# The delta rule's diagonal blocks inverted row by row on VectorE, and the heads' sums of squares as float32r rows

## The chip, the cores and the metric

The kernel runs on one core of a Trainium2 chip. The metric is the device time of one execution in microseconds (us); the execution before took 1631.58 us, the median of three. A core has the engines TensorE (PE: matrix products, and PEld, its loading of weights), VectorE (DVE), ScalarE (ACT), GpSimd (POOL) and SyncE (SP: it issues the loads of weights from memory). Each engine works through its own queue in a fixed order and waits for others on semaphores. PE writes its products to PSUM, all else lies in SBUF.

## The reference

Two layers of a hybrid block, then a second block of two (dilated attention with a short convolution, a gated feed-forward, retention, a second feed-forward). One sequence of 256 positions, model width 1024, all in float32. The change touches the mixer of the first block's two layers, which run over 16 + 256 = 272 positions:

```python
def gated_deltanet(q, k, v, z, a, b, conv_w, a_log, dt_bias, norm_g):
    qkv = jax.nn.silu(causal_dwconv(jnp.concatenate([q, k, v], axis=-1), conv_w))
    ...
    q = l2_norm(q.reshape(Bsz, T, A_HEADS, A_DK)) * (A_DK ** -0.5)
    k = l2_norm(k.reshape(Bsz, T, A_HEADS, A_DK))
    g = -jnp.exp(a_log.astype(f32)) * jax.nn.softplus(a.astype(f32) + dt_bias.astype(f32))
    ...
    decay = jnp.exp(jnp.where(incl, gcum[..., :, None] - gcum[..., None, :], -jnp.inf))
    kk = jnp.einsum('bhncd,bhnsd->bhncs', kc, kc)
    m = jnp.where(strict, bc[..., None] * kk * decay, 0.0)
    lhs = m + jnp.eye(CHUNK, dtype=f32)
    sol = lax.linalg.triangular_solve(lhs, rhs, left_side=True, lower=True, unit_diagonal=True)
    ...

def dsa_attention(q, k, v, iq, ik, iw, q_norm, k_norm, kidx_norm, cos_a, sin_a, cos_i, sin_i):
    q = apply_rope(rms_norm(q.reshape(Bsz, T, B_HEADS, B_DH), q_norm), cos_a, sin_a)
    k = apply_rope(rms_norm(k.reshape(Bsz, T, 1, B_DH), k_norm), cos_a, sin_a)[:, :, 0]
    ik = apply_rope(rms_norm(ik.reshape(Bsz, T, 1, IDX_DIM), kidx_norm), cos_i, sin_i)[:, :, 0]
    ...
```

So a layer needs, for every position, the sum of squares of 4 query heads and 4 key heads of the delta rule, 4 query heads and one key of the attention, and one index key: 14 sums. And for each of the 4 delta heads it needs the inverse of `I + m`, a unit triangular matrix, in each piece of the sequence. The kernel cuts the 272 positions into segments of 16, 128 and 128.

## The kernel before

**The stream.** Most of the time goes to products of activations with weights in float32r, a form of float32 with fewer bits kept. To keep float32's accuracy, weights and activations are split into a high and a low part, and `mm3` (L279) makes three products per 128 x 128 tile of weights: high x high (L287), high x low (L288), low x high (L289). `dense` (L291) loads weights (`raw`, 2 buffers), splits a block of 1024 columns with `split` (L259: ScalarE writes `whi`, VectorE `wlo`, 4 buffers each), and runs 24 products into one PSUM tile for every 128 output columns.

**The side chains.** Everything else in a mixer is written as generators: `small_chain` (decay gates, the index key), `key_chain` (the attention's key and value), `delta` (L917: `part1`, then `scan`, for the three segments) and `sparse` (top-k selection and attention). `dense` calls `tick` at its fourth tile and after each 128 output columns, and a tick lets every started chain go one step. What a chain issues thus stands in the engines' queues between products of the stream. A scheduler then fixes the order of each engine's queue. The order of the units of a layer is one line:

```python
for name in (begin + " k1 g1 q0 g2 q1 D i0 i1 S kv K v0 b0 v1 b1 g3 z0 z1 g4 g5 g6 g7").split():
```

`D` and `S` start the chains of the delta rule and of the attention, `M` the small chain, `K` the key chain; a chain waits with `until` for what it needs.

**The sums of squares.** `stats` (L493) squares a head on ScalarE (`sqm`, L496) and, two ticks later, multiplies each segment of it with a column of ones, in plain float32: three matmuls of one moving column into one PSUM tile `stat` (L500). The sums land one per partition (per position). A normalised value that is needed as a row across partitions goes through `rowcast` (L363). Each group of sums has its own Newton iteration for the inverse square root (`rsqrt`, L246: one start value and three rounds of three small VectorE instructions, L252 to L256).

**The inverse.** `part1` (L717) makes the decays (L723, L725), the matrix `MT` of a segment for 4 heads (L732, L735), and inverts it by levels: pairs (L739, L740), then two radix-4 steps of 2 and 8 rows (L764 to L776, with a transposition back of `XT` by L752 behind each), then the pair of 32 (L797 to L804), then the pair of 64 (L813, L818). Each product is four plain-fp32 matmuls, one per head. For the 16-row segment there is one radix step and the pair of 8. The 128-row segments are worked on in turn, after the 16-row segment's `scan`.

**How plain fp32 shows.** Each plain-fp32 matmul of the program is two records of the profile, one for each of its passes (a transposition is one). The stream's float32r products are one record.

## Time and profile before

| | |
|---|---|
| three runs | 1629.08, 1631.58, 1631.98 us |
| profiled execution | 1631.2 us, its span 1629.4 us |
| mean granted TensorE clock | 0.991 of full speed |
| PE busy | 1611.3 us, 11806 records |
| DVE busy | 1246.8 us, 2715 records |
| ACT busy | 890.1 us, 1556 records |
| GpSimd busy | 18.0 us |
| stretch read as layer 0's mixer | 25 to 277 us |

The span runs from the first instruction to the last; the execution's own time is a little longer. A row of the timeline gives the start, the duration, the engine, the line, the operation, and the names of what is written and read; equal neighbours are joined (x8). Matmuls are pipelined, so their durations overlap; what one costs is read from the distance of starts. Of the granted clock, 1.00 is the 2.4 GHz level and 0.50 the 1.2 GHz level.

### The profile page before, as it was taken

What the parts mean: (1) busy time and instruction counts of PE and PEld (TensorE: products, weight loads), DVE (VectorE), ACT (ScalarE), POOL (GpSimd) and SP (SyncE); (2) the same over time, 40 slices, a digit from 0 to 9 for tenths busy, and PEclk for the clock granted to TensorE, in tenths of its full rate; (3) what the DMA queues carried; (4) which work ended last, traced back from release to release, by engine and by line L of the source; (5) the groups of instructions that cost most, each with busy time, mean ns of one, the idle gap of its engine ahead of it and who ended that gap; (6) DMA issues with size and microseconds to landing.
All of it is one profiled execution on the core that took longest, in us unless ns stands there. A gap on an engine that the chain in (4) does not pass through costs nothing.

```text
span 1629.4 us, 30001 instructions
## 1 busy us (share of the span) xinstructions
PE 1611.3 (99%) x11806; PEld 1505.1 (92%) x11806; DVE 1246.8 (77%) x2715; ACT 890.1 (55%) x1556; POOL 18.0 (1%) x174
## 2 busy tenths in 40 slices
PE   7999999999999999999999999999999999999999
PEld 7989999999999989999998898899988888899997
DVE  6787568888557797588887649899956767789974
ACT  5665455555445664556665446566644444556652
POOL 0000000000000000000000000000000000000000
PEclk9998999999999999999999999999999999999999
DMA  5431224445553422245555553455555454545553
GB/s 207 155 110 73 104 99 161 169 171 179 169 181 130 155 104 79 79 147 170 193 191 179 200 180 126 160 182 188 185 183 194 158 178 155 174 169 192 190 183 128
DMA packets 38445, 257.89 MB, mean 158 GB/s; under 512 B 4384, under 2 KB 6816, under 8 KB 9120
## 3 DMA queue, kind: packets, MB, share of 16 engines
q1 hardware_dynamic: 37440, 253.79, 45.1%
q8 instruction: 93, 1.52, 0.4%
q10 hardware_dynamic: 864, 2.18, 0.3%
q14 instruction: 48, 0.39, 0.1%
HBM read 254.90 MB, written 1.05 MB: 157 GB/s over the span
## 4 chain that ended last, share of the span: by engine, by line
PE 96%; DVE 2%; ACT 1%; issue 0%; DMA 0%; SPq 0%; DVEq 0%; ACTq 0%
PE psd L289 20%; PE psd L287 19%; PE psd L288 18%; PE pss L285 5%; PE psn L285 5%; PE psd L285 3%; PE pss L289 3%; PE psn L289 3%; PE psn L771 1%; PE stat L500 1%; PE psd L352 1%; PE psd L353 1%; PE psd L354 1%; PE psn L353 1%; PE psn L352 1%; PE psn L354 1%
## 5 line engine op out<-in xcount | busy, mean ns | idle before, releaser
L261 ACT ACTIVATE whi<-raw 128x1024 fp32r<-128x1024 f32 (+1 forms) x487 | 508.3, 1044 | 546.6 <-PE psd L288 285.4
L262 DVE TENSOR_TENSOR wlo<-raw,whi 128x1024 fp32r<-128x1024 f32 (+1 forms) x487 | 585.2, 1202 | 206.9 <-ACT whi L261 202.6
L289 PE MATMUL psd<-x,wlo 128*128 128x256 f32 (+2 forms) x2384 | 682.5, 286 | 0.8 <-DVE wlo L262 0.8
L287 PE MATMUL psd<-x,whi 128*128 128x256 f32 (+2 forms) x2208 | 644.3, 292 | 7.0 <-ACT whi L261 6.3
L288 PE MATMUL psd<-x,whi 128*128 128x256 f32 (+2 forms) x2208 | 631.0, 286 | 0.0
L289 PEld LDWEIGHTS psd<-x,wlo 128*128 128x128 f32 x2384 | 451.9, 190 | 2.1 <-DVE wlo L262 1.3
L287 PEld LDWEIGHTS psd<-x,whi 128*128 128x128 f32 x2208 | 419.5, 190 | 15.7 <-ACT whi L261 6.3
L288 PEld LDWEIGHTS psd<-x,whi 128*128 128x128 f32 x2208 | 420.5, 190 | 3.0 <-issue 1.7
L289 PE MATMUL pss<-ax,wlo 128*128 128x256 f32 (+1 forms) x352 | 99.2, 282 | 0.0
L289 PE MATMUL psn<-ax,wlo 128*128 128x256 f32 (+1 forms) x352 | 99.2, 282 | 0.0
L285 PE MATMUL pss<-ax,whi 128*128 128x512 f32 x264 | 92.5, 394 | 0.0
L285 PE MATMUL psn<-ax,whi 128*128 128x512 f32 x264 | 92.5, 394 | 0.0
L289 PEld LDWEIGHTS psn<-ax,wlo 128*128 128x128 f32 x352 | 66.2, 188 | 0.0
L289 PEld LDWEIGHTS pss<-ax,wlo 128*128 128x128 f32 x352 | 66.2, 188 | 0.0
L285 PE MATMUL psd<-x,whi 128*128 128x512 f32 x176 | 61.7, 393 | 0.0
L285 PEld LDWEIGHTS pss<-ax,whi 128*128 128x128 f32 x264 | 49.6, 188 | 11.6
L285 PEld LDWEIGHTS psn<-ax,whi 128*128 128x128 f32 x264 | 49.6, 188 | 11.5
L389 ACT ACTIVATE gy<-gu,prm 128x256 f32<-128x256 f32 (+1 forms) x88 | 43.6, 500 | 4.0 <-DVE gu L386 3.8
L391 DVE SCALAR_TENSOR_TENSOR gy<-gu,prm,gy 128x256 f32<-128x256 f32 (+1 forms) x88 | 42.5, 485 | 1.7
L390 DVE SCALAR_TENSOR_TENSOR gy<-gu,prm,gy 128x256 f32<-128x256 f32 (+1 forms) x88 | 42.3, 483 | 0.9 <-ACT gy L389 0.9
L386 DVE TENSOR_TENSOR gu<-psd,rB 128x256 f32<-128x256 f32 (+2 forms) x88 | 37.0, 424 | 5.0 <-PE psd L289 3.7
L285 PEld LDWEIGHTS psd<-x,whi 128*128 128x128 f32 x176 | 33.0, 188 | 7.0
(404 smaller groups left out, 2497.2 us busy)
## 6 DMA issues: line engine op xcount, KB each, us to landing
raw<-in_w_up_dram SPq DMA_DIRECT2D x44, 1024.0 KB, 4.8
raw<-in_ffn_w_up_dram SPq DMA_DIRECT2D x44, 1024.0 KB, 4.7
raw<-in_w_in_dram SPq DMA_DIRECT2D x26, 1024.0 KB, 4.8
raw<-in_w_gate_dram SPq DMA_DIRECT2D x16, 1024.0 KB, 4.8
raw<-in_w_down_dram SPq DMA_DIRECT2D x16, 1024.0 KB, 4.9
raw<-in_ffn_w_down_dram SPq DMA_DIRECT2D x16, 1024.0 KB, 4.9
...
```

The source lines that it names most:

```text
L261: self.nc.scalar.activation(hi, src, AF.Copy)
L262: self.nc.vector.tensor_tensor(lo, src, hi.bitcast(F32), OP.subtract)
L285: mm(ps.rearrange("p (a n) -> p a n", a=2), w[0], x, start=first, stop=False)
L287: mm(ps, w[0], hi, start=first, stop=False)
L288: mm(ps, w[0], lo, start=False, stop=False)
L289: mm(ps[:, :n], w[1], hi, start=False, stop=last)
L352: mm(ps[m], h, hi[:, k, :], start=(kk == 0), stop=False)
L353: mm(ps[m], h, lo[:, k, :], start=False, stop=False)
L386: V.tensor_tensor(u[:, 2:2 + n], ps, N.rB, OP.mult)
L389: A.activation(y, u[:, o:o + T], AF.Copy, scale=conv(0, c))
L390: V.scalar_tensor_tensor(y, u[:, o + 1:o + 1 + T], conv(1, c), y, OP.mult, OP.add)
L391: V.scalar_tensor_tensor(y, u[:, o + 2:o + 2 + T], conv(2, c), y, OP.mult, OP.add)
```

## The change

**Sums of squares.** `square_parts` squares a head twice on ScalarE, to float32 and to float32r, and VectorE subtracts for a low part. The sum is then two float32r products of all 272 columns (`sums`), whose stationary matrix is a window of `pick` that has ones in one column and zeros elsewhere: the sum of head `r` lands in row `r` of a PSUM tile, and the other rows get zero added. Three sets a layer collect in the PSUM tile of bank x: `k5` (four keys and the index key), `q4` and `b5` (four attention queries and the attention key). When a set is full, ScalarE copies the rows out, and `columns` transposes the three segments (three transpositions a set). The Newton iterations become two of 15 columns. The index key's and attention key's factors are spread over partitions by `spread` (two float32r products of all-ones) in place of `rowcast`. A new chain `keys` starts with the small chain; the attention key is scaled later, in `sparse`.

**The inverse.** `delta` makes decays and `MT` of all three segments first. The 16 x 16 diagonal blocks of all 12 pairs of segment and head are gathered in one tile (`diag`: a mask, then a reduction on VectorE). `eliminate` scales them 15 times on ScalarE, spreads each column over its block's partitions with three products with the block mask (plain fp32), and runs 15 steps of a multiplication and a subtraction on VectorE, which invert all blocks at once. `part1` then starts from inverted blocks of 16: one radix-4 step of 16 rows and the pair of 64. For the 16-row segment the blocks are the result. The decay gates' sums take three matmuls, not six.

```diff
+    def square_parts(self, src, scale=1.0):
+        T = src.shape[1]
+        sq = self.st.tile([P, T1], F32, tag="sq", name="sqm", bufs=2)[:, :T]
+        hi, lo = self.part(T), self.part(T)
+        self.nc.scalar.activation(sq, src, AF.Square, scale=scale)
+        self.nc.scalar.activation(hi, src, AF.Square, scale=scale)
+        self.nc.vector.tensor_tensor(lo, sq, hi.bitcast(F32), OP.subtract)
+        return hi, lo
+    def sums(self, ps, w, hi, lo, first=True, last=True):
+        self.nc.tensor.matmul(ps, w, hi, start=first, stop=False)
+        self.nc.tensor.matmul(ps, w, lo, start=False, stop=last)
+    def spread(self, ps, cols, segs):
+        ns, T = len(segs), segs[-1][0] + segs[-1][1]
+        ch, cl = self.small(ns, "spr_h", F32R), self.small(ns, "spr_l", F32R)
+        self.nc.vector.tensor_copy(ch, cols)
+        self.nc.vector.tensor_tensor(cl, cols, ch.bitcast(F32), OP.subtract)
+        parts = []
+        for c in (ch, cl):
+            d = self.part(T)
+            for s, (o, n) in enumerate(segs):
+                self.nc.scalar.activation(d[:, o:o + n], self.c["ident"][:, :n], AF.Copy,
+                                          scale=c.bitcast(F32)[:, s:s + 1])
+            parts.append(d)
+        self.sums(ps[:, :T], self.ones, *parts)
...
-    stat = k_.ps("x", "stat")
-    SQ, SK, SA, SKA, SKI = 0, 12, 24, 36, 40
-    V.memset(stat[:, :43], 1.0)
     known = set()
-    def stats(src, rows, at, key):
-        sq = k_.st.tile([P, T1], F32, tag="sq", name="sqm", bufs=3)
-        A.activation(sq[:rows], src, AF.Square)
+    rows = {}
+    def stats(src, row, of, scale=1.0):
+        hi, lo = k_.square_parts(src, scale)
 
         def sums():
-            for s, (o, n) in enumerate(segs):
-                mm(stat[:n, at(s):at(s) + 1], sq[:rows, o:o + n], c["ones"][:rows, 0:1], start=True, stop=True)
-            known.add(key)
-        k_.defer(2, sums)
+            first = of not in rows
+            if first:
+                rows[of] = k_.ps("x", "rows")
+            rows["n", of] = rows.get(("n", of), 0) + 1
+            last = rows["n", of] == int(of[1])
+            k_.sums(rows[of][:, :T], k_.pick[:, P - 1 - row:2 * P - 1 - row], hi, lo, first, last)
+            if last:
+                t = tmp("rows")[:, :T]
+                A.activation(t, rows[of][:, :T], AF.Copy)
+                rows[of] = t
+                known.add(of)
+        k_.defer(3, sums)
+    def columns(of):
+        ps = k_.ps("s")
+        for s, (o, n) in enumerate(segs):
+            tr(ps[:, s * P:(s + 1) * P], rows[of][:, o:o + P], ident)
+        return ps[:, :3 * P].rearrange("p (s c) -> p s c", s=3)[:, :, :int(of[1])]
...
+    def keys():
+        yield from until("k5")
+        u = k_.small(15, "uki", bufs=2)
+        sums = columns("k5")
+        V.tensor_scalar(u[:, :12].rearrange("p (s h) -> p s h", s=3), sums[:, :, :4], 4.0 * EPS, None, OP.add)
+        V.scalar_tensor_tensor(u[:, 12:], sums[:, :, 4], 1.0 / 64.0, S["epu"], OP.mult, OP.add)
+        r = k_.rsqrt(u, 15, "rki")
+        uk = u[:, :12]
+        srk = k_.small(12, "srk", bufs=2)
+        V.tensor_tensor(srk, r[:, :12], uk, OP.mult)
+        yield
+        yield from until("small")
+        ruk = k_.small(12, "ruk")
+        V.reciprocal(ruk, uk)
+        bet = k_.small(12, "bet", bufs=2)
+        V.tensor_tensor(bet, S["beta"], ruk, OP.mult)
+        S["srk"], S["bet"] = srk, bet
+        known.add("bet")
...
+                stats(o, hh, "k5" if which == "k" else "q4")
...
+    diag = quad("vs", 2).rearrange("p h n -> p (h n)")[:, :12 * B].rearrange("p (h r) -> p h r", h=12)
+    slot = {0: 8, 1: 0, 2: 4}
...
+        own = diag[:, slot[s]:slot[s] + 4, :]
+        if s:
+            W = quad("W", 2)
+            V.tensor_tensor(W, MT, mid(c["blk"], 4), OP.mult)
+            V.tensor_reduce(own, W.rearrange("p h (b r) -> p h r b", r=B), AX.X, OP.add)
+        else:
+            G.memset(own, 0.0)
+            A.activation(own[:n], MT[:n], AF.Copy)
...
+    XD = dn.tile([P, 12, B], F32, tag="XD", name="XD")
+    def eliminate():
+        views = []
+        for tag, group in (("od", range(0, 3)), ("vt", range(3, 7)), ("ks", range(7, B - 1))):
+            low, o = quad(tag).rearrange("p h n -> p (h n)"), 0
+            for j in group:
+                m = B - 1 - j
+                views.append(low[:, o:o + 12 * m].rearrange("p (h r) -> p h r", h=12))
+                A.activation(views[j], diag[:, :, j + 1:], AF.Copy, scale=c["idb"][:, j:j + 1])
+                o += 12 * m
+            ps = k_.ps("n")
+            mm(ps[:, :o], c["blk"], low[:, :o], start=True, stop=True)
+            A.activation(low[:, :o], ps[:, :o], AF.Copy)
+            yield
+        V.tensor_copy(XD, mid(c["idb"], 12))
+        Y = quad("Y", 2).rearrange("p h n -> p (h n)")
+        for j in range(B - 1):
+            m = B - 1 - j
+            t = Y[:, :12 * m].rearrange("p (h r) -> p h r", h=12)
+            V.tensor_tensor(t, views[j], XD[:, :, j:j + 1].to_broadcast([P, 12, m]), OP.mult)
+            V.tensor_tensor(XD[:, :, j + 1:], XD[:, :, j + 1:], t, OP.subtract)
+            if j % 3 == 2:
+                yield
...
+    def part1(s):
+        o, n = segs[s]
+        E4, DT, MT = S["E4"], DTs[s], MTs[s]
+        own = XD[:, slot[s]:slot[s] + 4, :]
+        if s:
+            XT, Xm = quad("XT", 2), quad("X", 2)
+            V.tensor_tensor(XT.rearrange("p h (b r) -> p h b r", r=B),
+                            own.unsqueeze(2).to_broadcast([P, 4, NB, B]),
+                            c["blk"].rearrange("p (b r) -> p b r", r=B).unsqueeze(1).to_broadcast([P, 4, NB, B]),
+                            OP.mult)
...
-        yield from until("small", *[(w, hh) for w in "qk" for hh in range(4)])
-        uqk = k_.small(24, "uqk", bufs=2)
-        V.tensor_scalar(uqk, stat[:, :24], 4.0 * EPS, None, OP.add)
-        uk = uqk[:, 12:24]
-        rk = k_.rsqrt(uk, 12, "rk")
-        srk = k_.small(12, "srk", bufs=2)
-        V.tensor_tensor(srk, rk, uk, OP.mult)
-        ruk = k_.small(12, "ruk")
-        V.reciprocal(ruk, uk)
-        bet = k_.small(12, "bet", bufs=2)
-        V.tensor_tensor(bet, S["beta"], ruk, OP.mult)
+        yield from until("bet", "q4")
         epo = k_.small(12, "epo", bufs=2)
-        V.tensor_scalar(epo, uqk[:, 0:12], 16.0 * EPS * 128.0, None, OP.mult)
-        S["srk"], S["bet"], S["epo"] = srk, bet, epo
-        yield
+        V.tensor_scalar(epo.rearrange("p (s h) -> p s h", s=3), columns("q4"), 4.0 * EPS, 16.0 * EPS * 128.0,
+                        OP.add, OP.mult)
+        S["epo"] = epo
+        yield
+        yield from in_turn(decays(0), decays(1), decays(2))
+        yield from eliminate()
         yield from part1(0)
...
-             "M": lambda: k_.start(small_chain()), "K": lambda: k_.start(key_chain())}
+             "M": lambda: (k_.start(small_chain()), k_.start(keys())), "K": lambda: k_.start(key_chain())}
```

**Where the instructions go.** Three places are shown, before and now.

On PE, early in layer 0, the sum of the index key's squares before, as it stands in the stream (`stat` is the tile of sums, `x_...` and `psd` are the stream's):

```order
L288 MATMUL psd<-x_119,whi 128x272
L289 MATMUL psd<-x_119,wlo 128x272
L500 MATMUL stat<-g_77,sqm 16x1
L500 MATMUL stat<-g_77,sqm 128x1 x2
L173 MATMUL pss<-g_77,sacc 16x1
L173 MATMUL pss<-g_77,sacc 128x1 x2
L287 MATMUL psd<-x_98,whi 128x272
L288 MATMUL psd<-x_98,whi 128x272
```

and the end of the first set now, with the low part's product (L279) and the three transpositions (L550, `columns`):

```order
L324 MATMUL psd<-x_103,whi 128x272
L325 MATMUL psd<-x_103,whi 128x272
L279 MATMUL rows<-sqp,pick 128x272
L326 MATMUL psd<-x_103,wlo 128x272
L324 MATMUL psd<-x_106,whi 128x272
L325 MATMUL psd<-x_106,whi 128x272
L326 MATMUL psd<-x_106,wlo 128x272
L324 MATMUL psd<-x_109,whi 128x272
L325 MATMUL psd<-x_109,whi 128x272
L326 MATMUL psd<-x_109,wlo 128x272
L324 MATMUL psd<-x_112,whi 128x272
L550 MATMUL pss<-g_82,rows 128x128 x3
```

A group of plain-fp32 matmuls stands between two float32r products before; now a product of the stream's own shape stands there, and a group of three transpositions once in a set.

On PE, where the 16-row segment of layer 0 is inverted before (`XT` the inverse so far, `MT` the matrix):

```order
L288 MATMUL psd<-x_113,whi 128x256
L289 MATMUL psd<-x_113,wlo 128x256
L752 MATMUL psn<-g_77,XT 16x16 x4
L287 MATMUL psd<-x_116,whi 128x256
L288 MATMUL psd<-x_116,whi 128x256
L289 MATMUL psd<-x_116,wlo 128x256
L764 MATMUL psn<-X,MT 16x16 x4
L287 MATMUL psd<-x_119,whi 128x256
```

and now, at the products with the block mask (L831; `od`, `vt`, `ks` hold the scaled columns, L707 are index scores):

```order
L707 MATMUL pss<-ikT,iq_1009 128x128
L831 MATMUL psn<-od,g_98 128x504
L707 MATMUL pss<-ikT,iq_1009 128x128
L324 MATMUL psd<-x_103,whi 128x272
L831 MATMUL psn<-vt,g_98 128x504
L325 MATMUL psd<-x_103,whi 128x272
```

Eight such groups of the 16-row segment are gone, and three wide products stand at one place.

On DVE, between two low parts of weights (`wlo`) before, the 16-row segment's steps (L765 to L776) with the index queries' rotation (L623 to L625):

```order
L262 TENSOR_TENSOR wlo<-raw,whi 128x1024
L765 TENSOR_TENSOR Y<-psn,g_93 16x4x16
L623 TENSOR_TENSOR iq_1094<-psd,g_93 128x256
L624 TENSOR_TENSOR iqb<-iqb,g_93 128x256
L775 TENSOR_TENSOR W<-XT,psn 16x4x2x4
L625 TENSOR_TENSOR iq_1094<-iq_1094,iqb 128x256
L776 TENSOR_TENSOR XT<-XT,psn 16x4x2x2
L262 TENSOR_TENSOR wlo<-raw,whi 128x1024
L775 TENSOR_TENSOR W<-XT,psn 16x4x2x2
L776 TENSOR_TENSOR XT<-XT,psn 16x4x2x2
```

and now between two low parts, during the elimination (L839, L840; L712 are index scores, L718 and L719 the top-k selection):

```order
L299 TENSOR_TENSOR wlo<-raw,whi 128x1024
L840 TENSOR_TENSOR XD<-XD,Y 128x12x10
L712 SCALAR_TENSOR_TENSOR ix_1228<-ix_1227,aabw,ix_1228 128x128
L839 TENSOR_TENSOR Y<-vt,XD 128x108
L712 SCALAR_TENSOR_TENSOR ix_1228<-ix_1227,aabw,ix_1228 128x128
L840 TENSOR_TENSOR XD<-XD,Y 128x12x9
L718 MAX m_1372<-ix_1228 128x8
L839 TENSOR_TENSOR Y<-ks,XD 128x96
L719 MATCH_REPLACE ix_1228<-m_1372,ix_1228 128x128
L840 TENSOR_TENSOR XD<-XD,Y 128x12x8
L718 MAX m_1372<-ix_1228 128x8
L839 TENSOR_TENSOR Y<-ks,XD 128x84
```

The piece now is the start of 27 instructions that stand between that `wlo` and the next one. Before, six stand between the two shown.

## Rows read from the trace of the kernel before

**Rows 1.** Page: busy time, granted clock by slice, chain by engine

```profile
PE 1611.3 (99%) x11806; PEld 1505.1 (92%) x11806; DVE 1246.8 (77%) x2715; ACT 890.1 (55%) x1556; POOL 18.0 (1%) x174
...
PEclk9998999999999999999999999999999999999999
...
PE 96%; DVE 2%; ACT 1%; issue 0%; DMA 0%; SPq 0%; DVEq 0%; ACTq 0%
```

**Rows 2.** Waits of PE: line, awaited, us in total, times, longest

```profile
PE psd L287 <- ACT o L261: 1.3, 1, 1.3
PE psd L289 <- DVE wlo L262: 0.8, 1, 0.8
```

**Rows 3.** Windows: us, each engine's busy us, PEclk, DMA share, GB/s

```profile
60.00:100.00 40.00, 40.00 (x363) 36.89 (x361) 31.12 (x91) 25.17 (x54) 0.48 (x5) 1.00 0.41 144
100.00:120.00 20.00, 20.00 (x153) 17.61 (x152) 19.38 (x65) 14.05 (x29) 0.20 (x2) 1.00 0.23 84
```

**Rows 4.** Timeline, a `wlo` and its first use, twice: start us, us

```profile
126.46 1.21 DVE L262 TENSOR_TENSOR wlo<-raw,whi 128x1024 fp32r<-128x1024 f32 x1
...
128.90 0.29 PE L289 MATMUL psd<-x,wlo 128*128 128x272 f32 x1
...
594.29 1.21 DVE L262 TENSOR_TENSOR wlo<-raw,whi 128x1024 fp32r<-128x1024 f32 x1
...
601.38 0.29 PE L289 MATMUL psd<-x,wlo 128*128 128x260 f32 x1
```

**Rows 5.** Timeline of PE, one set of sums of squares (L500)

```profile
67.06 0.29 PE L289 MATMUL psd<-x,wlo 128*128 128x272 f32 x1
67.28 0.74 PE L500 MATMUL stat<-g,sqm 128*16 128x1 f32 x6
...
68.09 0.29 PE L288 MATMUL psd<-x,whi 128*128 128x272 f32 x1
```

**Rows 6.** PE by form, layer 0's mixer: count, busy us, mean ns, idle

```profile
L771 PE MATMUL psn<-XT,Y 128*128 128x96 f32 x32 | 4.0, 272 | 0.0
...
L752 PE MATMUL psn<-g,XT 128*128 128x128 f32 x24 | 3.3, 272 | 0.0
...
L578 PE MATMUL psn<-g_g,g 16*128 16x4 f32 x6 | 1.1, 258 | 0.0
...
L764 PE MATMUL psn<-X,MT 16*16 16x16 f32 x8 | 0.4, 173 | 0.0
```

**Rows 7.** Timeline of PE, one group of eight records (L771)

```profile
157.17 1.03 PE L771 MATMUL psn<-XT,Y 128*128 128x96 f32 x8
...
158.19 0.29 PE L288 MATMUL psd<-x,whi 128*128 128x272 f32 x1
```

**Rows 8.** Timeline of PE, a 512-column fp32 product in retention

```profile
1267.39 1.02 PE L1374 MATMUL pss<-v,a 128*128 128x512 f32 x2
...
1268.48 0.39 PE L353 MATMUL psd<-wlo,x 128*128 128x512 f32 x1
1268.71 0.39 PE L354 MATMUL psd<-whi,x 128*128 128x512 f32 x1
```

**Rows 9.** DVE by form, layer 0's mixer

```profile
L262 DVE TENSOR_TENSOR yl<-ya,yh 128x272 fp32r<-128x272 f32 x8 | 3.5, 440 | 0.0
...
L725 DVE SCALAR_TENSOR_TENSOR QT<-psn,g_ngc,g 128x128 f32<-128x128 f32 x8 | 2.7, 337 | 1.5 <-PE psn L723 1.5
...
L765 DVE TENSOR_TENSOR Y<-psn,g 128x512 f32<-128x512 f32 x4 | 2.8, 688 | 0.5 <-PE psn L764 0.5
...
L255 DVE TENSOR_TENSOR nwt_b<-nwt_a,uqk 128x12 f32<-128x12 f32 x3 | 0.5, 156 | 0.0
```

**Rows 10.** Timeline of DVE, two instructions that don't depend on each other

```profile
82.08 0.15 DVE L254 SCALAR_TENSOR_TENSOR nwt_a<-rk_y 128x12 f32<-128x12 f32 x1
82.16 0.41 DVE L624 TENSOR_TENSOR iqb<-iqb,g 128x256 f32<-128x256 f32 x1
```

**Rows 11.** Windows, the stretch behind the wait at 128 us

```profile
133.20:143.20 10.00, 10.00 (x45) 8.70 (x44) 4.92 (x16) 3.66 (x14) 0.00 (x0) 0.50 0.31 107
```

More of the change, by code (lines that the diff above doesn't have):

```diff
@@ L34 @@
 SEGS3 = [(0, 4), (4, 128), (132, 128)]
[L35 removed]
+B = 16
+NB = P // B
 def _rope(T, dim):
@@ L585, in small_chain @@
         known.add("small")
+    def keys():
[17 more added lines that the diff above has]
+        yield
+        ps = k_.ps("s")
+        k_.spread(ps, r[:, 12:], segs)
+        ikg, iks, ikT = tmp("ikg")[:, :T], tmp("iks")[:, :T], big("ikT")
+        V.scalar_tensor_tensor(ikg[:64], smT[:64], col["kidx"][:64, :], ps[:64, :T], OP.mult, OP.mult)
+        A.activation(ikg[64:], ikg[:64], AF.Copy)
+        for q in range(4):
+            f = 32 if q % 2 == 0 else 0
+            A.activation(iks[32 * q:32 * q + 32], ikg[f:f + 32], AF.Copy)
+        yield
+        V.tensor_tensor(ikT, ikg, c["cosI"], OP.mult)
+        V.tensor_tensor(iks, iks, c["sinI"], OP.mult)
+        V.tensor_tensor(ikT, ikT, iks, OP.add)
+        S["ikT"] = ikT
+        known.add("ikT")
     cv = {}
@@ L635, in index @@
         ikT = S["ikT"]
+        two = [mp.tile([P, 2, SEQ], F32, tag=f"pT{j}", name=f"ix{j}") for j in range(2)]
+        rls, scs = [two[0][:, j, :] for j in range(2)], [two[1][:, j, :] for j in range(2)]
         for hh in range(8):
@@ L673, in key_chain @@
     def key_chain():
-        yield from until("ka", "va")
-        ua = k_.small(3, "uka")
-        V.scalar_tensor_tensor(ua, stat[:, SKA:SKA + 3], 1.0 / P, S["epu"], OP.mult, OP.add)
-        ra = k_.rsqrt(ua, 3, "rka")
-        yield
-        pr = k_.ps("s")
-        for s in range(3):
-            k_.rowcast(pr, ra[:, s:s + 1], segs[s])
-        V.tensor_tensor(kT, kT, pr[:, :T], OP.mult)
-        yield
+        yield from until("va")
         x = S["vraw"]
@@ L740, in part1 @@
-        V.tensor_tensor(XT[:n, :, :n], XT[:n, :, :n], mid(ident[:n, :n], 4), OP.add)
         yield
-        Xm = quad("X", 2)
-        def cols(t, w, a0, a1):
-            v = t[:n, :, :n].rearrange("p h (b c) -> p h b c", c=4 * w)
-            return v[:, :, :, a0 * w:a1 * w]
-        def untranspose(m):
-            p3 = heads(k_.ps("n"))
-            for hh in range(4):
-                tr(p3[:m, hh, :m], XT[:m, hh, :m], ident[:m, :m])
-            A.activation(Xm[:m, :, :m], p3[:m, :, :m], AF.Copy)
@@ new lines, in part1, with cols, untranspose @@
+    def part1(s):
[8 more added lines that the diff above has]
+                            OP.mult)
+            def cols(t, a0, a1):
+                v = t.rearrange("p h (b c) -> p h b c", c=4 * B)
+                return v[:, :, :, a0 * B:a1 * B]
+            def untranspose(m):
+                p3 = heads(k_.ps("n"))
+                for hh in range(4):
+                    tr(p3[:m, hh, :m], XT[:m, hh, :m], ident[:m, :m])
+                A.activation(Xm[:m, :, :m], p3[:m, :, :m], AF.Copy)
+            untranspose(n)
+            yield
@@ L1008, in sparse @@
     def sparse():
-        yield from until(*[("iq", t) for t in range(4)])
+        yield from until("ikT", *[("iq", t) for t in range(4)])
         yield from index(0)
         yield from index(1)
-        yield from until("kv", *[("bq", hh) for hh in range(4)])
-        uq = k_.small(12, "uqa")
+        yield from until("kv", "b5")
+        uq = k_.small(15, "uqa")
         e128 = k_.small(3, "e128")
         V.tensor_scalar(e128, S["epu"], float(P), None, OP.mult)
-        V.tensor_tensor(uq.rearrange("p (s c) -> p s c", s=3),
-                        stat[:, SA:SA + 12].rearrange("p (s c) -> p s c", s=3), bc(e128, 4), OP.add)
-        qsc = k_.rsqrt(uq, 12, "qsc", bufs=2)
+        sums = columns("b5")
+        V.tensor_tensor(uq[:, :12].rearrange("p (s c) -> p s c", s=3), sums[:, :, :4], bc(e128, 4), OP.add)
+        V.tensor_tensor(uq[:, 12:], sums[:, :, 4], e128, OP.add)
+        qsc = k_.rsqrt(uq, 15, "qsc", bufs=2)
         nqs = k_.small(12, "nqs", bufs=2)
-        V.tensor_scalar(nqs, qsc, -1.0, None, OP.mult)
+        V.tensor_scalar(nqs, qsc[:, :12], -1.0, None, OP.mult)
+        rk = k_.small(3, "rka")
+        V.tensor_scalar(rk, qsc[:, 12:], math.sqrt(P), None, OP.mult)
+        yield
+        ps = k_.ps("s")
+        k_.spread(ps, rk, segs)
+        V.tensor_tensor(kT, kT, ps[:, :T], OP.mult)
         yield
```

116 lines of the change are left out of this document (37 added, 79 removed).

## The prediction

> **What bounds the kernel now.** I read the page's busy times and its chain of waits first. TensorE (PE) is busy 99% of the span and is 96% of the chain that ended last [rows 1]. The view of PE's waits says the same from the other side: besides the start there is little, and VectorE's (DVE) low halves `wlo` cost 0.8 us in the whole run [rows 2]. So a microsecond off PE's stream is a microsecond off the end, as long as the other engines keep up. The third view is therefore DVE by stretches of time. Over the run it is 77% busy, but while the side chains of a mixer run it is not: 31.12 us of 40 between 60 and 100 us, then 19.38 of 20 [rows 3]. The fourth is how far ahead the splits are. The 31st low half ends at 127.67 us (126.46 + 1.21), and the first product of its block starts at 128.90: 1.2 us ahead, the smallest up to there once the start is over. In layer 1 it is at least 601.38 - 594.29 - 1.21 = 5.9 [rows 4]. The forecast is thus a sum on PE and a second one on DVE.
>
> **PE, part by part.** A price is the time that a group of plain-fp32 instructions pushes the float32r stream back: from the matmul before it to the second one behind it, less two spacings of 0.125 us.
>
> - Sums of squares. A group of six records cost 68.09 - 67.06 - 0.25 = 0.78 us [rows 5]. There are 14 sets a layer, 28 groups, 21.8 us; about six adjoin other fp32 work and share the switch, so 20.6. In their place stand 56 float32r products of 272 columns; their shape is that of the stream, 0.125 us each, 7.0. Net -13.6.
> - Two 128-row segments a layer. The rows by form of layer 0 give the busy time that goes [rows 6]: half of four forms, L764's and three of L771, each with 32 records and near 4.0 us (7.9 together); all of L797 and L803, of the same kind with 16 records each (3.8); 8 of the 24 records of L752 (1.1): 12.8 us a layer, 25.6 for two. Busy records overlap their neighbours: a group shown as 1.03 us pushed the stream by 158.19 - 157.17 - 0.125 = 0.9 [rows 7], and the groups of the two segments often adjoin. I take -23; the ends are 20 and 25.6.
> - The 16-row segment. Six product groups go each layer, each of 8 records and 0.4 us [rows 6], and two of transposes at half of that or a little more: 2.9, twice, -5.8.
> - Row casts. Four groups of six records, 128 columns wide and read by me like those of [rows 7], 0.9 to 1.0, become 8 float32r products of 0.125: -2.8. The sums of the decay gates fall from six matmuls to three: half of L578's 1.1 us and as much of its sister L579, in each layer [rows 6]: -2.0.
> - Added: six sets of three transposes, at 3.3 us for 24 (L752) [rows 6]: 18 x 0.14 = +2.5. Three products a layer with the block mask, 504, 504 and 432 columns in fp32, which no row shows: the nearest is one of 512 columns in retention, 1268.48 - 1267.39 = 1.09 up to the second product behind it, less the stage's spacing of 1268.71 - 1268.48 = 0.23: 0.86 [rows 8]; six, +5.2. The ends are 0.39 each (what the stream's own 512-column product takes there) and 1.09.
>
> Sum: -13.6 - 23 - 5.8 - 2.8 - 2.0 + 2.5 + 5.2 = **-39.5 us**. No DMA is added or moved, and GpSimd only fills a few constants and clears smaller tiles. From the ends of the mixers, where PE waits for the branches' last heads (1.3 us in layer 1 on ScalarE's `o` [rows 2]), I take another 2, because the delta chain has fewer links.
>
> **DVE, up to the 31st split.** Its queue is in a fixed order: a `wlo` stands behind whatever the scheduler put ahead of it, and PE's stream stands behind `wlo`. The order of the changed kernel moves these ahead of the 31st split of a layer:
> - decays and products of both 128-row segments, 16 instructions of 0.337 us [rows 9]; a neighbour that doesn't depend on the one ahead starts before that one ends (82.08 + 0.15, the next at 82.16) [rows 10], so 0.26 each, 4.2;
> - the block mask over 512 columns twice, 0.69 by L765 [rows 9], and two reductions of 512 elements to 64 that no row shows; the nearest pass over 512 is L765 too, less the shared edge 0.6, with ends of 0.4 and 1.0: 2.6 in all;
> - thirteen low parts of squares, each like L262's on 272 columns, 0.44 less 0.08 [rows 9]: 4.7;
> - one more group of value or query filters and top-k steps that slide ahead: 1.5 + 2.6;
> - the elimination. 30 instructions, 2 x 12 x (15 + ... + 1) = 2880 elements. A 12-element one takes 0.156 and a 272-element one 0.44 [rows 9], so about 1.09 us per 1000 elements (3.1), and the rest is fixed: 0.07 each if every one overlaps an independent neighbour (2.1), 0.14 each if none does (4.3). 5.2 to 7.4; the order puts score and top-k instructions between them, so I take 5.2.
>
> That is 21 us. Gone from ahead of it are two of three Newton chains (2.4 us, by ten instructions of about 0.16 that half overlap) and the 16-row segment's radix steps (1.1). Net **+17.5 us**.
>
> The errata section of the Trainium skill's "VectorE: DVE Perf Modes" speaks against this part: an SBUF instruction pays a fixed latency, so many small tiles pay it each time, and its formula for fp32 tensor_tensor, (N + 151)/0.96 ns, makes 7.7 us a layer of the elimination (an estimate). The rows agree on the size of a lone instruction (0.156 for 12 elements) but show the overlap with independent neighbours, so I stay with 5.2; by the page the sum below would be 5 us later.
>
> How much of 17.5 reaches PE: the idle DVE time between 60 and 100 us is 40 - 31.12 = 8.9 us [rows 3], spent behind full split buffers; the decays, masks and part of the low parts fall there, and I let them fill 7.5 of it. PE gets there 2.5 us sooner, for the fp32 groups that have gone by then. Layer 0: 17.5 + 2.5 - 7.5 - 1.2 (the lead) = 11.3. Layer 1, with a lead of 5.9 and taken to have as much idle time: 6.6. Together **+17.9 us** of PE waiting for `wlo`, in a bracket from 0 (all absorbed) to 36 (elimination at 7.4, reductions near 1 us, no idle time filled).
>
> Afterwards DVE has slack again (the scans fall where it was half busy), so the stall isn't paid twice. ScalarE gets 28 more squares at 0.4, 48 small copies and 30 scaled ones, some 25 us net over two mixers; it runs at 55% [rows 1], and what stands behind it is `whi`. I take nothing for that. New waits: the transposes of a set of sums stand in PE's queue behind ScalarE's copy of the rows, with 5 to 8 stream products (0.6 to 1.0 us) between, and the mask products behind its scaled copies; whatever waits there holds the whole stream. A copy that gets behind a `whi` comes too late by up to 0.8, twelve times: 0 to 10, and I take +2. If ScalarE's cover for `whi` is gone, 3 more.
>
> **Sum.** The profiled execution took 1631.2 us (span 1629.4), 0.4 below the runs' median, so no correction. 1631.2 - 39.5 - 2 + 17.9 + 2 = 1609.6, **1610**.
>
> **Rivals.**
> 1. PE stays the only bound: the four split buffers take all DVE work. For it: PE waited 0.8 us for `wlo` in all of before. Against: that one wait came exactly where the lead was used up [rows 2, 4]. 1631.2 - 39.5 - 2 + 2 = 1592.
> 2. DVE sets the pace in both mixers' middles: each added instruction counts in full and dependent ones don't overlap. 17.5 + 2 (elimination at 7.4) a layer, less the leads, plus 2.5: 2 x 22 - 7 = 37, less 4 of idle time: 33; 1631.2 - 39.5 - 2 + 33 + 2 = 1625. For it: 19.38 of 20 [rows 3]. Against: the idle 8.9 us before it.
> 3. Slower: the stalls drop the clock. In before, PE waited 0.8 us at 128, and from 133.2 to 143.2 its granted clock was 0.50, the 1.2 GHz level, with PE busy throughout [rows 11]; such a stretch costs about half its length, 5 us. If six further ones follow the waits of rival 2 or of the forecast, +30 on 1610: 1640. It decides from about 50 us more at the half clock. Against: the row of granted clocks is near full in all of before [rows 1], though PE waits at the mixers' ends too. The Trainium skill's "TensorE: Matmul & The Clock Gate", Part 1, ties the gate to recent activity; by that rule short stalls spread over a stage could cost more than their length, which is this rival; the trace bears out one stretch of it in a mixer.
>
> **Chances.** Forecast 0.50 (own range 1600 to 1620), rival 1 0.22, rival 2 0.20, rival 3 0.08. A measurement of this kernel tells 0.2% (3.3 us): 1628.3 to 1634.8 is "the same", in reach of rival 2's upper end and rival 3's lower: 0.06. Faster 0.87, slower 0.07. The range runs from rival 1 less a few to rival 2 plus a few: **1589 to 1629**.
>
> **What would show it.** Right: PE's records fall by about 430; the waits view has PE on `wlo` (L299 now) with 10 to 25 us, nearly all in two stretches of 30 us around the elimination, and DVE busy over 19 of 20 us there; no group of plain fp32 remains at the sums; DVE's own total moves by less than 10 us, since what it gains early it loses in the 128-row segments. Wrong on DVE: that wait stays under 4 us (rival 1), or passes 30 (rival 2). Wrong on PE: its busy time without waits falls by less than 33, because the float32r products or the mask products cost more than their nearest rows. Wrong on the clock: more than 50 us at 0.50 beyond before's.

## The result and the profile after

The changed kernel took 1614.01 us (median of four, 1610.02 to 1616.36) against 1630.33 for the kernel before on the same chip: ratio 0.9897, 95% interval 0.9874 to 0.9921. The forecast was 1610 in a range of 1589 to 1629. The profiled execution took 1613.39 us; its span is 1611.6.

The page of the changed kernel, to be read beside [rows 1]: busy times, granted clock by slice, and the chain by engine (lines between are left out, "...").

```profile
PE 1582.0 (98%) x11360; PEld 1470.3 (91%) x11360; DVE 1257.3 (78%) x2727; ACT 912.8 (57%) x1640; POOL 16.5 (1%) x173
...
PEclk9998999999999989999999999999999999999999
...
PE 86%; DVE 8%; ACT 4%; DMA 1%; issue 1%; SPq 0%; DVEq 0%; ACTq 0%
```

PE has 446 records fewer and is busy 29.3 us less, but the span is only 17.8 us shorter. The difference of span and busy time, PE's idle time, went from 1629.4 - 1611.3 = 18.1 to 1611.6 - 1582.0 = 29.6 us. The chain of waits says the same: VectorE holds 8% of it now, not 2%, and ScalarE 4%, not 1%.

PE's waits after the change, to be read beside [rows 2] (awaited, us in total, times, longest):

```profile
PE psd L324 <- ACT whi L298: 6.3, 1, 6.3
PE rows L278 <- ACT sqp L272: 2.9, 5, 1.6
PE psd L324 <- DVE xp L661: 2.6, 3, 1.7
PE psd L326 <- DVE wlo L299: 2.5, 3, 1.0
PE psn L831 <- ACT od L828: 1.2, 2, 0.8
PE pss L169 <- DVE sacc L163: 1.1, 1, 1.1
PE psn L831 <- ACT vt L828: 0.9, 1, 0.9
```

No name dominates: the first row is the start, as before; then squares that a sum waits for, evictions of the stream's PSUM tiles (`xp`), low halves (`wlo`), scaled copies ahead of the mask products. Of these rows the first 20 us hold, besides the first, the longest wait for a square (1.6 us; before, PE waited 2.0 us there for the index key's `sqm`), the norm's sum (`sacc`), and the longest for `wlo` (1.0). The two other waits for `wlo`, 1.4 us together, stand between 120 and 140 us, around the elimination.

The same stretches as [rows 3] and the one behind them (busy us of PE, PEld, DVE, ACT, POOL, then the granted clock):

```profile
60.00:100.00 40.00, 38.43 (x290) 34.55 (x289) 37.64 (x93) 32.69 (x79) 0.41 (x4) 1.00 0.32 106
100.00:120.00 20.00, 19.96 (x142) 16.71 (x142) 19.45 (x76) 12.84 (x29) 0.20 (x2) 1.00 0.17 54
120.00:140.00 20.00, 17.37 (x109) 14.34 (x106) 20.00 (x52) 11.75 (x26) 0.00 (x0) 0.90 0.30 106
```

The idle 8.9 us of VectorE between 60 and 100 us are 2.4 now, and from 120 to 140 us it has none, while PE is idle 2.6 us there.

How a sum looks now, to be read beside [rows 5] (timeline of PE: start, duration, line):

```profile
119.15 0.29 PE L325 MATMUL psd<-x,whi 128*128 128x272 f32 x1
119.28 0.29 PE L278 MATMUL rows<-sqp,pick 128*128 128x272 f32 x1
119.41 0.28 PE L279 MATMUL rows<-sqp,pick 128*128 128x272 f32 x1
119.53 0.29 PE L324 MATMUL psd<-x,whi 128*128 128x272 f32 x1
```

The two products (L278, L279) stand in the stream at its own spacing of 0.125 us, 0.25 us for a sum that cost 0.78.

**A common measure for the runs below.** I priced each matmul by the distance from its start to the next start, with one price list for all kernels here (for each pair of kinds and widths the 30th percentile of the distances at 2.4 GHz). The list's sum is PE's own work; what goes over it at full clock is waiting; what goes over it at 1.2 GHz is the clock. Some 11 us of each span, ahead of the first matmul and behind the start of the last, are in no column.

| | own work | waiting | half clock |
|---|---|---|---|
| before | 1583.5 | 22.4 | 13.0 |
| sums alone | 1569.0 | 35.0 | 10.7 |
| inverse alone | 1559.4 | 26.9 | 10.3 |
| changed | 1545.5 | 40.4 | 14.6 |
| without steps | 1544.3 | 36.1 | 7.7 |
| steps doubled | 1544.3 | 46.8 | 12.0 |

Changed against before: -38.0, +18.0 and +1.6 us, together -18.4 of the span's -17.8.

Only differences are read from this table: its levels hang on how pairs are sorted and on the percentile. A second list from the same traces, at the same percentile, sorts pairs by their full shapes and by whether they read a split part. It has 1541.6, 63.9 and 13.5 for before, 1505.5, 79.8 and 15.3 for the changed kernel: -36.1, +15.9 and +1.8. For the sums alone it gives -12.6 of own work and +10.9 of waiting, for the inverse alone -21.7 and +2.2. So a difference is good to 2 or 3 us.

### The profile page after: what moved, and what is told of

Its sections match the earlier page's. It is cut to its first block, busy times and chain, and to the rows that moved or that the text cites. A ratio compares the mean times of both kernels' runs of the same rounds, so it can differ in the third digit from the quotient of the medians.

```text
span 1611.6 us, 29157 instructions
## 1 busy us (share of the span) xinstructions
PE 1582.0 (98%) x11360; PEld 1470.3 (91%) x11360; DVE 1257.3 (78%) x2727; ACT 912.8 (57%) x1640; POOL 16.5 (1%) x173
## 4 chain that ended last, share of the span: by engine, by line
PE 86%; DVE 8%; ACT 4%; DMA 1%; issue 1%; SPq 0%; DVEq 0%; ACTq 0%
PE psd L326 18%; PE psd L324 16%; PE psd L325 16%; PE pss L322 5%; PE psn L322 5%; PE psd L322 3%; PE pss L326 3%; PE psn L326 3%; DVE wlo L299 2%; PE psd L389 1%; PE psd L391 1%; PE psd L390 1%; DVE yv L666 1%; PE psn L390 1%; PE psn L389 1%; PE psn L391 1%
## 5 line engine op out<-in xcount | busy, mean ns | idle before, releaser
L324 PEld LDWEIGHTS psd<-x,whi 128*128 128x128 f32 x2208 | 420.5, 191 | 20.5 <-ACT whi L298 6.3
L325 PEld LDWEIGHTS psd<-x,whi 128*128 128x128 f32 x2208 | 422.0, 191 | 4.0 <-issue 2.6
L427 DVE SCALAR_TENSOR_TENSOR gy<-gu,prm,gy 128x256 f32<-128x256 f32 (+1 forms) x88 | 42.5, 485 | 0.9 <-ACT gy L426 0.9
L451 DVE TENSOR_TENSOR a<-vy,s 128x256 f32<-128x256 f32 (+1 forms) x88 | 37.5, 426 | 2.6 <-ACT s L437 0.6
```

Of the source, the lines that this page charges most:

```text
L324: mm(ps, w[0], hi, start=first, stop=False)
L325: mm(ps, w[0], lo, start=False, stop=False)
L427: V.scalar_tensor_tensor(y, u[:, o + 1:o + 1 + T], conv(1, c), y, OP.mult, OP.add)
L451: V.tensor_tensor(a, y, G[m], OP.mult)
```

## The experiments

Times are medians of 4 to 11 runs, ratios are to the kernel before on the same chip.

**1. The sums of squares alone, 2. the inverse alone.** The changed kernel with the inverse of before, and the other way round. (The cuts show the lines that matter, without the methods and constants that go with them; comments with a run's number are added.)

```diff
-        yield from in_turn(decays(0), decays(1), decays(2))   # 1: and part1, constants of before
-        yield from eliminate()
```
```diff
+        yield from in_turn(decays(0), decays(1), decays(2))   # 2: in before, with the new part1
+        yield from eliminate()
```

To make room for 48 columns of the second, a small tile of gates has one buffer in place of two.

> The change's sums of squares with the inverse of before (pairs, radix 2 and 8, pairs of 32 and 64). By the PE prices of the prediction: sums -13.6, row casts -2.8, gate sums -2.0, transposes +2.5, together -15.9 us. Theory A (VectorE's queue: what stands ahead of the low halves sets PE's waits): VectorE gets only 13 low parts more and two Newton chains less, net about +2 us a layer, so waits rise by 1 to 3 us and the time is 1616 to 1618. Theory B (the new links: PE waits for ScalarE's second squares, its copy of the rows, and the transposes behind it, whatever VectorE has to do): most of the new waits come with the sums, +7 or more, 1622 or later.

> The change's elimination with the sums of squares of before. PE prices: -23 (128-row segments) -5.8 (16-row segment) +5.2 (mask products) = -23.6 us. Theory A: the decays, masks, reductions and 30 steps, some 13 us of VectorE a layer, come with it, so most of the waits do too: +10 to +14, 1617 to 1621. Theory B: only the mask products' wait for scaled copies comes with it, +2 to +4: 1609 to 1612.

Sums alone: 1627.20 us, ratio 0.9978 (0.9969 to 0.9986). Inverse alone: 1612.23 us, ratio 0.9895 (0.9879 to 0.9911). PE's own work came as priced (-14.5 and -24.1 us). The waits came the other way round: +12.6 with the sums, +4.5 with the inverse. Theory A fails for both. Theory B holds for the sums, and for the inverse but for a little: 4.5 us where it had at most 4. At equal granted clock the halves differ more plainly. At 0.992 the kernel before took 1628.65 to 1630.39 us on this chip and the sums alone 1627.34 to 1628.09; at 0.993 the inverse alone took 1609.67 and 1609.85 and the changed kernel 1610.02 in the measurement above. So the sums' half gains 1 or 2 us by itself and nothing visible beside the inverse: its new waits eat what it saves on PE.

The places tell more. PE and VectorE around the elimination (100 to 140 us) and in its counterpart in layer 1; first before, then the changed kernel, two rows each:

```profile
100.00:140.00 40.00, 39.79 (x280) 34.79 (x280) 35.37 (x110) 26.39 (x62) 0.20 (x2) 0.91 0.27 95
540.00:600.00 60.00, 60.00 (x503) 54.63 (x502) 53.95 (x169) 40.10 (x86) 0.41 (x4) 1.00 0.35 124
100.00:140.00 40.00, 37.33 (x248) 31.04 (x247) 39.45 (x127) 24.58 (x55) 0.20 (x2) 0.95 0.23 80
540.00:600.00 60.00, 56.50 (x382) 47.85 (x381) 56.30 (x167) 46.23 (x112) 0.40 (x4) 0.95 0.29 103
```

the sums alone:

```profile
100.00:140.00 40.00, 39.78 (x292) 34.98 (x291) 37.29 (x110) 29.40 (x68) 0.20 (x2) 0.96 0.28 103
540.00:600.00 60.00, 59.31 (x458) 53.50 (x457) 55.21 (x145) 45.43 (x102) 0.40 (x4) 1.00 0.36 125
```

the inverse alone:

```profile
100.00:140.00 40.00, 38.40 (x258) 33.29 (x257) 35.75 (x126) 21.02 (x47) 0.20 (x2) 0.91 0.26 93
540.00:600.00 60.00, 56.57 (x400) 48.62 (x400) 54.68 (x176) 38.44 (x93) 0.30 (x3) 0.97 0.26 88
```

PE is idle 0.9 us there with the sums and 5.0 with the inverse (0.2 before). Where the new chain of keys runs it is the other way; before and the changed kernel:

```profile
40.00:60.00 20.00, 20.00 (x148) 19.64 (x149) 15.10 (x24) 10.53 (x17) 0.20 (x2) 0.91 0.44 159
480.00:540.00 60.00, 59.19 (x476) 56.48 (x475) 45.51 (x115) 33.54 (x59) 0.90 (x11) 1.00 0.43 155
40.00:60.00 20.00, 18.34 (x151) 17.77 (x150) 16.43 (x47) 13.23 (x28) 0.20 (x2) 1.00 0.57 201
480.00:540.00 60.00, 56.97 (x435) 54.47 (x435) 50.23 (x140) 36.88 (x73) 0.61 (x6) 0.94 0.36 125
```

the sums alone:

```profile
40.00:60.00 20.00, 17.99 (x147) 16.75 (x145) 16.54 (x44) 13.06 (x26) 0.20 (x2) 1.00 0.57 204
480.00:540.00 60.00, 55.65 (x455) 52.47 (x454) 47.84 (x140) 35.83 (x71) 0.90 (x11) 0.94 0.41 140
```

the inverse alone:

```profile
40.00:60.00 20.00, 20.00 (x158) 19.37 (x157) 14.63 (x30) 9.65 (x18) 0.30 (x3) 1.00 0.45 159
480.00:540.00 60.00, 59.75 (x487) 57.04 (x487) 47.50 (x130) 36.76 (x68) 0.70 (x7) 1.00 0.41 140
```

6.4 us idle with the sums, 0.2 with the inverse (0.8 before). So there are two places, and each half of the change brings one.

The longest wait at the keys' place can be followed in the sums alone:

```profile
57.08 0.49 DVE L644 SCALAR_TENSOR_TENSOR ikg<-smT,prm,pss 64x272 f32<-64x272 f32 x1 [0.88 <-PE pss L283]
58.58 1.23 DVE L303 TENSOR_TENSOR wlo<-raw,whi 128x1024 fp32r<-128x1024 f32 x1
60.08 0.43 DVE L665 TENSOR_TENSOR xp<-psd,rB 128x272 f32<-128x272 f32 x1
60.57 0.39 PE L328 MATMUL psd<-x,whi 128*128 128x272 f32 x1 [2.45 <-DVE xp L665]
```

`xp` empties a PSUM tile of the stream. In VectorE's queue it stands behind the index key's `ikg`, which waits for the spreading products (`pss`), and behind a `wlo`; PE's stream stands 2.45 us until it is done. In the changed kernel the wait at this place is 1.7 us, for `xp` (L661) again. A new link and VectorE's fixed order thus act together here.

**3. Without the steps, 4. steps doubled.** Run 3 has the 30 step instructions of a layer left out, run 4 has them twice (the second pair into scratch). The lines in question:

```diff
-            V.tensor_tensor(t, views[j], XD[:, :, j:j + 1].to_broadcast([P, 12, m]), OP.mult)
-            V.tensor_tensor(XD[:, :, j + 1:], XD[:, :, j + 1:], t, OP.subtract)
```

> The changed kernel without the 30 multiplications and subtractions of the elimination (its blocks stay the identity, so the inverse is not computed). Nothing else is left out. Theory A: VectorE's queue is shorter by 5.2 us a layer ahead of the 31st split; two thirds or more of that reach PE: 6 to 10 us faster than the changed kernel, 1604 to 1608. Theory B: no link of PE hangs on these steps (the first use of the result is far behind), at most 2 us faster, 1612.

> The changed kernel with every one of the 15 multiplications and subtractions done twice (the second pair into scratch): 30 more VectorE instructions a layer, 5 to 7.5 us. Theory A: each microsecond counts now that the lead is gone: +10 to +15 us, 1624 to 1629. Theory B: +0 to +3, 1614 to 1617.

Without: 1602.34 us, ratio 0.9826 (0.9813 to 0.9839). Doubled: 1619.30 us, ratio 0.9931 (0.9918 to 0.9944). Around the elimination, without the steps:

```profile
100.00:140.00 40.00, 39.32 (x294) 34.38 (x293) 37.23 (x109) 30.26 (x74) 0.20 (x2) 1.00 0.31 106
540.00:600.00 60.00, 58.27 (x424) 49.88 (x423) 52.74 (x139) 47.18 (x118) 0.40 (x4) 1.00 0.32 107
```

with doubled steps:

```profile
100.00:140.00 40.00, 34.73 (x228) 28.53 (x226) 39.44 (x147) 22.32 (x52) 0.20 (x2) 0.91 0.24 80
540.00:600.00 60.00, 52.78 (x363) 45.09 (x363) 56.67 (x184) 40.36 (x98) 0.40 (x4) 0.97 0.29 98
```

PE's idle time at this place is 2.4 us without, 6.2 in the changed kernel (2.7 + 3.5), 12.5 with doubled steps; at the keys' place (20 to 100 us, and 480 to 540) it is 7.8, 6.3 and 6.3. Around the elimination the mechanism of theory A holds: PE waits for what VectorE has in its queue. Its size does not: it had 6 to 10 us less without the steps and 10 to 15 more with double ones, and the waits moved by 4.3 and 6.4. The 11.7 us of run 3 are more than its waits: 6.9 of them are time at the half clock (14.6 to 7.7). Nor does the wait go by the name `wlo`. With doubled steps the waits view of the whole run has

```profile
PE psd L326 <- DVE wlo L299: 4.2, 5, 1.3
PE psn L913 <- DVE v L670: 2.7, 3, 1.4
```

1.7 us more for `wlo` than the changed kernel, 2.1 more for `v`, and the rest under other names.

**5. High parts only.** The sums alone, with one square and one product a sum.

```diff
-        self.nc.scalar.activation(sq, src, AF.Square, scale=scale)
-        self.nc.vector.tensor_tensor(lo, sq, hi.bitcast(F32), OP.subtract)
-        self.nc.tensor.matmul(ps, w, lo, start=False, stop=last)
```

> The kernel with the sums of squares alone (sums_alone, 1627.2 us; its stream's own price is 14.4 us below before's, its waits are 12.4 above), now with only the high part of the squares: the second square on ScalarE, the subtraction on VectorE and every second product of a sum are left out (28 each), so the sums are rounded. Theory L (load: what the sums give VectorE and ScalarE to do makes PE wait): -3.5 for 28 products and -6 or more of the waits, 1617 or less. Theory K (links: the waits sit where the new chain of keys puts its transposes, Newton steps, spread and index key, and at the start): the waits stay within 2 us, 1622 to 1625.

1622.12 us, ratio 0.9946 (0.9933 to 0.9958): 5.1 us below the sums alone, of which 3.7 are PE's own work. The waits fell by 0.8 us (35.0 to 34.2) though VectorE's busy time fell by 8.7. Theory L, by which 6 us or more of the waits go, fails; the time lies in theory K's range.

**6. Keys later, 7. low parts on GpSimd, 8. five ticks.**

```diff
-        yield                       # 6, in keys(), ahead of spread
+        for _ in range(3):
+            yield
-        self.nc.vector.tensor_tensor(lo, sq, hi.bitcast(F32), OP.subtract)    # 7
+        self.nc.gpsimd.tensor_tensor(lo, sq, hi.bitcast(F32), OP.subtract)
-        k_.defer(3, sums)           # 8
+        k_.defer(5, sums)
```

> The changed kernel with two more steps of the chain between the Newton iteration of the keys and the spreading of its factors (the products with all-ones then stand about 25 stream products later in PE's queue in layer 0). Theory K: PE's waits at this place (1.9 us in layer 0, 2.3 in layer 1) go, 3 to 5 us faster than the changed kernel: 1609 to 1611. Theory L: VectorE has as much ahead as before, the waits move to another name: within 1.5 us of 1614.

> The changed kernel with the low parts of the squares subtracted on GpSimd, which is busy 1% of the span, instead of VectorE (28 instructions of 0.44 us, some 5 us a layer). Theory L: VectorE's queue gets 4.7 us a layer shorter, half or more reaches PE: 5 to 8 us faster than the changed kernel, 1606 to 1609, if GpSimd takes under about 1 us for one. Theory K: within 2 us of 1614; slower if GpSimd takes so long that the sums wait for it.

> The changed kernel with the sums' products issued 5 ticks behind the squares instead of 3. The waits of a sum's first product for its square (2.9 us in all, 5 of them) go. If that were all, 1611. Theory K: as the sets are full later, the chain of keys and the delta rule start later, and the place of keys keeps its waits: 1610 to 1614. Theory L: within 2 us of 1614.

1610.56 us, ratio 0.9869 (0.9851 to 0.9887); 1611.34, 0.9876 (0.9857 to 0.9894); 1606.04, 0.9843 (0.9826 to 0.9860). All three medians are below the changed kernel's 1614.01, but only run 8's interval is clear of its (0.9874 to 0.9921). Run 6 lies in theory K's range, run 7 between the theories, run 8 below both. The waits explain little of it: they were 38.5, 42.3 and 42.1 us against 40.4. Run 8 did not even shorten the waits that it was aimed at: PE waits 3.2 us for squares, not 2.9, of which 1.6 stand in the first 20 us, as in the changed kernel. Keys later cleared 40 to 60 us (idle 1.7 to 0.0) and PE's idle time between 60 and 140 us rose (4.2 to 5.9). With GpSimd the sums wait for GpSimd; the waits of run 7:

```profile
PE rows L279 <- POOL xp L660: 5.1, 7, 1.0
PE rows L279 <- POOL sqp L273: 3.5, 5, 1.7
```

What run 8 gained over the changed kernel in its profiled execution is the clock (14.6 to 3.6 us at the half clock). Clocks differ between executions of one kernel: run 8's took 1601.39 us at a mean of 0.998 and 1607.34 at 0.992, the changed kernel's 1616.36 at 0.988 and 1610.02 at 0.993. At 0.994 and 0.993 the two are 1606 and 1610, so some 3 us are left that are not the clock (a thousandth of it is about 1.3 us, by run 10 below), and they are not in the waits either; PE's own work (1543.3 against 1545.5) may be 2 of them, within what the list can tell.

**9. The sums alone with both delays, 10. the changed kernel with both, 11. five ticks and GpSimd.** Edits of 6 to 8, combined.

> The sums of squares alone (sums_alone, 1627.2 us, waits 12.4 us above before's) with the sums' products 5 ticks behind the squares instead of 3, and two more steps of the chain of keys ahead of the spreading. No engine does less or more. Theory K (the waits hang on links that are issued too early): 5 us or more of the 12.4 go, 1622 or less. Theory L (they hang on how much VectorE and ScalarE have to do): within 2 us of 1627.

> The changed kernel with both: 5 ticks and two more steps ahead of the spreading. Alone they gave 1606.0 and 1610.6 against 1614.0. Theory K: they ease two links, so they add in part: 1602 to 1605. If the second only moves what the first has moved already: 1606.

> The changed kernel with 5 ticks and the low parts on GpSimd, where one took 1.04 us and PE waited for it 8.6 us in all with 3 ticks. With 5 ticks that wait goes. Theory L for what is left: VectorE has 4.7 us a layer less in front of its low halves of weights, 1599 to 1602. Theory K alone: no more than 5 ticks alone give, 1605 to 1607.

1624.68 us, ratio 0.9957 (0.9945 to 0.9970); 1608.37, 0.9854 (0.9832 to 0.9876); 1611.00, 0.9874 (0.9859 to 0.9889). Run 9 got back 3.5 us of 12.6 (waits 31.5), between the theories. Runs 10 and 11 give nothing beyond run 8 and lie above what either theory had for them; their waits are 42.5 and 47.0. Run 10 at one time took 1599.76 us at a clock of 0.998, at another 1611.51 at 0.989.

**12. The index key as before.** Its own sum, Newton iteration and row cast again, so that the chain of keys ends with its four heads.

```diff
-        stats(smT, 4, "k5", c["blk2"][:, 0:1])
+        A.activation(sq[:64], smT[:64], AF.Square)
+        k_.defer(2, isums)
+        yield from until("ik")
...
+            k_.rowcast(ps, ri[:, s:s + 1], segs[s])
```

> The changed kernel with one part undone: the index key's sum, Newton iteration and row cast are made as before (three plain-fp32 products, a chain of its own in the small chain, ahead of the other keys), so that the chain of keys waits for four sums, runs 12 columns, and has no spreading and no index key behind it. PE's own price rises by 2 x (0.78 + 0.96 - 4 x 0.125) = 2.5 us. Theory K': the place of keys (40 to 60 us, 480 to 540 us), where the changed kernel waits 6 us more than before, waits for this chain; 5 us or more of that go, so 1609 to 1612. Theory L: VectorE has the same instructions and a Newton iteration more, the waits stay: 1616 to 1618.

1623.06 us, ratio 0.9931 (0.9913 to 0.9950): 9 us slower than the changed kernel, and 5 to 6 us at an equal clock of 0.989 (1619.48 against 1613.39 and 1614.63). Its windows at the keys' place:

```profile
20.00:40.00 20.00, 19.09 (x135) 18.03 (x133) 15.28 (x62) 10.72 (x20) 0.10 (x1) 0.93 0.46 159
40.00:60.00 20.00, 16.95 (x110) 16.86 (x110) 14.45 (x30) 9.96 (x20) 0.30 (x3) 0.83 0.32 109
480.00:540.00 60.00, 58.04 (x453) 56.37 (x453) 51.35 (x145) 36.83 (x68) 0.82 (x10) 0.97 0.42 142
```

and its waits:

```profile
PE psd L324 <- DVE gz L1147: 5.4, 2, 3.6
```

Theory K' fails, and the time lies above theory L's too. PE's idle time between 60 and 100 us and from 480 to 540 us shrank (1.6 to 0.7, 3.0 to 2.0), but from 20 to 60 us it grew (1.7 to 4.0): PE waits there for an eviction of the stream (`gz`, 3.6 us), which stands in VectorE's queue behind the end of the earlier chain, filters and two `wlo`. The sum of waits is 41.7 us, 1.3 more than with the change; PE's work is 3.2 more, and the half clock 5.2 more (4.1, 0.3 and 5.2 by the second list).

Of the runs with the whole change, run 8 is faster than the changed kernel; 6, 7, 10 and 11 have lower medians, with intervals that meet its. Run 2 equals it without the sums' half.

## Why the prediction came out right

- **PE's own work: right.** Forecast -39.5, measured -38.0: the sums' half -14.5 (forecast -13.6 - 2.8 - 2.0 + 2.5 = -15.9), the inverse's -24.1 (forecast -23 - 5.8 + 5.2 = -23.6). The mask products, which no row had shown, are 1.1, 1.0 and 0.9 us of busy time each against 0.86; the transposes 3.2 us against 2.5.
- **The new waits: right in size, wrong in cause.** Forecast +17.9 for `wlo`, +2 for new links, -2 at the mixers' ends; measured +18.0 (+15.9 by the second list). The forecast had them wait for `wlo`, in two stretches around the elimination, and that step failed: `wlo` is 2.5 us in the whole run, 1.4 of them around the elimination and 1.0 in the start. That is under the 4 us which the prediction had named as a sign of being wrong on VectorE. Runs 1 and 2 put 12.6 of the waits on the sums' half and 4.5 on the inverse's, where my VectorE sum had 12 of 21 us a layer on the inverse and 4.7 on the low parts of squares. Halving the sums' work moved the waits by 0.8 us (run 5), so most of the sums' 12.6 are not the price of that work. The +2 for links was the term that was too small, and the +17.9 for VectorE's queue the one too large: of 6.2 us idle around the elimination 3.8 went with the steps (run 3). The right total is luck, a coincidence of the two errors. The lead of the splits was used up around the elimination, as forecast, but PE waited little there; the longest:

```profile
120.21 1.21 DVE L299 TENSOR_TENSOR wlo<-raw,whi 128x1024 fp32r<-128x1024 f32 x1
121.47 0.39 PE L326 MATMUL psd<-x,wlo 128*128 128x272 f32 x1 [0.87 <-DVE wlo L299]
```

- **The -2 at the mixers' ends: right as far as the view tells.** The 1.3 us for ScalarE's `o` [rows 2] are gone from the changed kernel's waits.
- **The row of `wlo` before was misread.** Rivals 1 and 3 have PE wait 0.8 us for `wlo` at 128 us, where the lead was used up. The row stands in the start:

```profile
17.35 0.60 PE L289 MATMUL psd<-x,wlo 128*128 128x272 f32 x1 [0.76 <-DVE wlo L262]
```

  Between 20 and 400 us the view of PE's waits before has 0.5 us in all, none for `wlo`. So this row does not speak against rival 1, and the stretch at 1.2 GHz from 133 us, on which rival 3 rests, did not follow such a wait.
- **What VectorE adds: its durations were right.** The changed kernel's rows in layer 0, to be read beside [rows 9] (count, busy us, mean ns):

```profile
L273 DVE TENSOR_TENSOR sqp<-sqm,sqp 128x272 fp32r<-128x272 f32 x13 | 5.7, 436 | 0.1
L810 DVE TENSOR_REDUCE vs<-W 128x64 f32<-128x512 f32 x2 | 2.1, 1042 | 0.0
L840 DVE TENSOR_TENSOR XD<-XD,Y 128x180 f32<-128x180 f32 x1 | 0.3, 344 | 0.0
L839 DVE TENSOR_TENSOR Y<-ks,XD 128x12 f32<-128x12 f32 x1 | 0.2, 169 | 0.0
```

  Only the reduction is past its upper end (1.04, bounds 0.4 to 1.0, 0.6 taken). Leaving the steps out took VectorE's busy time from 1257.3 to 1246.6 us, 5.35 a layer for a forecast of 5.2. The formula in the Trainium skill's "VectorE: DVE Perf Modes" (the section on the errata) makes 345 and 170 ns of 180 and 12 elements, an estimate that the last two rows bear out (344 and 169). But 7.7 us a layer, the estimate for 30 of them one after the other, isn't what they cost in a queue of other work: 5.35, because neighbours overlap, as in [rows 10].
- **What reaches PE of it: overrated.** 10.7 us of steps fewer gave 3.8 us less idle time at their place, and 10.1 more gave 6.3. I had let VectorE's idle time fill 7.5 us a layer and counted the rest in full. VectorE did fill up, to 2.4 us idle between 60 and 100 us and 19.45 and 20.00 of 20 us behind that, as the prediction had it; its own total rose by 10.5 us, a little more than the 10 named there.
- **Rival 1** (all hidden, 1592) fails by 16 to 18 us of waits, though few of them are for `wlo`. **Rival 2** is out by size. **Rival 3** did not come: the stretches at the half clock are 3.4 us, 10.2, 6.8, 3.4 and 10.2 in the changed kernel. They add up to 34.0 us against 27.2 before, and cost 14.6 against 13.0. But the clock is no small thing here: it moves one kernel by up to 12 us between executions (run 10), more than any of runs 6 to 12 moved the median.
- **What stays open** is what makes the sums' 12.6 us up, beyond the wait for `xp` that the trace shows (2.45 us in the sums alone). Runs 5 to 12 eased the amount of work, the delay of the sums, the place of the spreading, and the index key, one at a time and in pairs. Run 6 cleared the stretch that it was aimed at and run 12 parts of it, run 8 did not, and the waits stood elsewhere afterwards: 38.5 to 47.0 us in all of them that have both halves of the change, 31.5 at best with the sums alone. Whether the stream's lead in split weights is what all of these draw on isn't shown: more buffers for them weren't tried.
